# Modulation vectors of a two-block network: column groups of 1024, with the sums over the partitions begun by 32x32 transposes on VectorE

## The chip, the cores and the metric

One core of a Trainium2 chip runs the whole program in one launch. The time is the device time of one execution in microseconds (us), and the median of the runs counts. The engines are named as in the profile: PE is TensorE's matmul, PEld its weight load, DVE is VectorE, ACT is ScalarE, POOL is GpSimd, SP is SyncE, whose queue issues all the loads of weights.

## What is computed

The reference is a two-block residual network on 256 tokens of x (and 256 tokens of a context) with 1024 features, all in float32. Before every mixing or feed-forward stage the input is normalised and then modulated by vectors that come from a conditioning vector:

```
m = silu(cond) @ w_mod + b_mod          # first block: [1024] x [1024, 3072]
shift, scale, gate = split(m, 3)        # second block: [1024] x [1024, 9216], two layers, 9 vectors each
pre(h) = rms_norm(h, gain) * (1 + scale) + shift
h = h + gate * mixer(pre(h))
```

There are two conditioning vectors, one for x (`c`, `c_2`) and one for the context (`c_ctx`, `c_ctx_2`), so each product has two rows. The first block mixes with a chunked gated delta rule in both directions and a pooling branch. The second block has, for each of two layers, a feed-forward part (`ffn`, weight 0.5 on its gate), a mixer (a short convolution in layer 0, latent attention in layer 1) and another feed-forward part. The context leaves the computation after layer 1's attention has read its keys and values, so the last four modulation vectors of layer 1, and the gate of the first block, are used for x alone.

## The kernel before, in words

Activations lie transposed: features on the partitions, tokens in the free dimension (256 of x, then 256 of the context). A float32 product is made of three products of two-part operands (`mm3`, lines 220 to 223), each part `float32r`; every weight chunk of 128 x 2048 float32 (1 MB) is loaded as it is (`wraw`) and split into two parts (`whl`) by ACT (line 150) and DVE (line 151).

The work is a list of steps in `Program` (lines 64 to 155), each with the chunks that it uses. `pump` hands out raw buffers and split buffers in the order of the steps. In the second block there are two raw buffers (`wraw`) and four pairs of split buffers. A chunk that is not split, as those of `w_mod` are, keeps its raw buffer until its step has read it. After that a planner (the Tile framework's scheduler, line 1874) puts the instructions of each engine in an order by readiness in its own model of times; each engine then runs its own list in that order.

The modulation vectors are made by `mod_group` (lines 257 to 310), 512 columns at a time. A group is two steps, one per 512 rows of `w_mod`, so one 1 MB chunk each. A step runs in one of two ways:

- `by_pe` (lines 261 to 278): 16 products of 128 columns, with silu(c) as 32 stationary columns; four of them lie side by side in the array. The second step copies the sums to SBUF on ACT (tile `modsb`) and transposes them on PE, and two small DVE instructions add the bias.
- `by_dve` (lines 280 to 307): the products are left as 128 partial sums on the partitions. For each of four rows of weights and both conditioning vectors a `scalar_tensor_tensor` of 512 columns multiplies and adds into `macc` (the first two of a group are done by ACT, line 289). The second step then sums over the partitions on PE with four products of `ones` (line 298, tile `ps_mod`), copies to SBUF on ACT (line 300, `modsb`), transposes twice on PE (line 303, tile `ps_tr`) and adds the bias with two small DVE instructions (line 307).

PSUM has eight banks (line 171): four for products (`mm`), two that fill in (`fl`), one for small things (`tr`) and one for modulation (`mod`). The bank `mod` is also taken by the sums of the queries' squares in the first block (`T["ssq"]`, line 941, held from `q_step` 0 to `q_rows`) and by the second block's norms.

`mod_steps` (lines 349 to 357) takes the next steps from the queue `mod_q` and puts them into the list. There are 76 of them: 4 of the first block's gate and 72 of the second block. They are put

- two behind the solver of the first block (line 935) and ten into the scan over x (line 1142), by PE;
- one behind each `up` step of a feed-forward part whose context is still there (line 1392) and behind every second `down` step of its first half (line 1365), by DVE, until eight are left: 56 steps, in 28 groups;
- the last eight into the attention (line 1707), by PE.

An `up` step (lines 1317 to 1329) is 48 products of 512 columns into two banks, whose evacuation (`evac_g`, lines 1293 to 1299) uses the tiles `fs` and `fg` with two buffers each. A `z_step` of the first block (lines 999 to 1006) is 24 products into a bank `fl`; its result goes to the tile with the tag `X`, which was the scratch of the query steps before it (`Yw`, lines 967 and 968).

Of the kernel before, what the change touches and what calls it, by code (L numbers as in the profile page):

```python
# [14 lines left out]
P = 128  # L15
# [11 lines left out]
# columns of the packed per-feature vectors  # L27
# [12 lines left out]
class Chunk:  # L40
    """A piece of a weight matrix: n columns of float32 per partition, as the matrix product
    takes them (raw) or split into two float32r parts."""
# [7 lines left out]
class Slices:  # L50
    """A pool of [128, 256] tiles in slices of one tile."""
# [12 lines left out]
class Program:  # L64
    """Steps in their order, each with the weight pieces it uses; the pieces are loaded and split
    ahead of the steps, as far as there are buffers."""
# [10 lines left out]
    def add(self, fn, *chunks, lead=False):  # L77
        """lead: the step's instructions come before the splits that have room with it."""
        self.steps.append((fn, chunks, lead))
# [29 lines left out]
    @contextmanager  # L109
    def queued(self, behind):  # L110
        """Instructions that come behind these on their engines."""
        with ExitStack() as order:
            for ins in behind:
                order.enter_context(self.tc.issue_after(ins))
            yield
# [43 lines left out]
def adaln_net(ctx: ExitStack, tc: tile.TileContext, I, out):  # L159
# [13 lines left out]
    def bank(tag="mm"):  # L173
        """A bank by its use: products, fillers between them, small things, modulation;
        in the second block the first two in turn."""
# [33 lines left out]
    def into_row(h):  # L209
        """[128, 128], ones in the columns 64 + h and 96 + h: sums over partitions into those rows."""  # L210
        return rowsel[:, 7 - h:7 - h + P]

    def from_row(r):
        """[128, 128], ones in the row r: spreads that row over all partitions."""
        return ident[:, r:r + 1].to_broadcast([P, P])
# [41 lines left out]
    def mod_group(src, czt, dst, bias):  # L257
        """512 columns as 2 steps, one per 512 rows of w_mod."""
        st = {}

        def by_pe(c, ch):
# [3 lines left out]
            for k in range(4):  # L265
                for j in range(4):
                    o = k * 512 + j * P
                    mm(ps[32 * j:32 * j + 32, 0:P], czt[:, 4 * c + k, :], ch.raw[:, o:o + P],
                       c == 0 and k == 0, c == 1 and k == 3)
            if c == 0:  # L270
                return
            sb = const.tile([P, S], F32, tag="modsb", name="modsb")
            nc.scalar.activation(out=sb[:, 0:P], in_=ps[:, 0:P], func=AF.Copy)
            tr = side_bank()
            transpose(tr[:, 0:P], sb[:, 0:P])
            i0 = tr[:, 0:P].rearrange("p (j s) -> p j s", s=32)
            for r in range(2):
                tt(dst[:, :, r], i0[:, :, r], bias, ALU.add)

        def by_dve(c, ch):  # L280
            if c == 0:
                st["acc"] = T["scr"].tile([P, 2, 512], F32, tag="macc", bufs=1, name="macc")
            acc = st["acc"]
            for k in range(4):
                w = ch.raw[:, k * 512:(k + 1) * 512]
                for r in range(2):
                    cv = czt[:, 4 * c + k, r:r + 1]
                    if c == 0 and k == 0:
                        nc.scalar.activation(out=acc[:, r, :], in_=w, func=AF.Copy, scale=cv)  # L289
                    else:  # L290
                        stt(acc[:, r, :], w, cv, acc[:, r, :], ALU.mult, ALU.add)
            if c == 0:
                return
            ps = bank("mod")
            for r in range(2):
                for j in range(2):
                    q = 32 * (2 * r + j)
                    mm(ps[q:q + 32, 0:S], ones[:, 0:32], acc[:, r, j * S:(j + 1) * S])
# [5 lines left out]
            i0 = tr[:, 0:S].rearrange("p (b r j s) -> p r j b s", b=2, r=2, s=32)  # L304
            o = dst.rearrange("p (j b) r -> p j b r", b=2)
            for r in range(2):
                tt(o[:, :, :, r], i0[:, r, :, :, 0], bias.rearrange("p (j b) -> p j b", b=2), ALU.add)

        for c in range(2):
            mod_q.append((c, by_pe, by_dve, st, Chunk(src[c], 2048, split=False)))  # L310

    def mod_first(g):
        """Shift and scale of two tiles of the features."""
# [29 lines left out]
    for j in range(2):  # L343
        mod_group(I["w_mod_b"][j], cz["1"], mods["1"][:, 16 + 4 * j:20 + 4 * j], vec("b_mod", 16 + 4 * j, 4))
    for i in range(2):
        for j in range(18):
            mod_group(I["w_mod2"][i, j], cz["2"], mods[f"2{i}"][:, 4 * j:4 * j + 4], vec("b_mod_2", 72 * i + 4 * j, 4))
# [11 lines left out]
    def token_sums(out_, x, start, stop):  # L359
        """Sums over the partitions of x [128, 128], by tokens on the partitions: a column."""  # L360
        mm(out_, x, ones[:, 0:1], start, stop)

    def by_token(out_, r):
        """Columns of r, one per 128 tokens, over all partitions with the tokens in a row."""
# [1514 lines left out]
```

## Time and profile before

| | |
|---|---|
| runs | 2118.60, 2118.64, 2121.05 us; median 2118.64 us |
| profiled execution: span from first to last instruction | 2119.8 us; its time with what lies around the span is not listed apart |
| PE busy | 2077.7 us, 98% |
| PEld busy | 1797.6 us, 85% |
| DVE busy | 1266.4 us, 60% |
| ACT busy | 840.3 us, 40% |
| POOL busy | 77.4 us, 4% |
| DMA | 311.74 MB, mean 147 GB/s |
| chain that ended last, by engine | PE 95%, DVE 2%, ACT 1%, DMA 1%, issue 1% |
| mean granted TensorE clock | 0.994 |

The busy times are unions of the instructions' durations on each engine. [...] The chain of waits follows the last instruction back to what released it; its pieces are given in order of time, each with its start and its length.

### The profile page before, as it was taken

The numbers are of one execution on the slowest core, as the hardware profiler recorded it, in microseconds if no ns is written. First come the engines' busy times: TensorE is split into PE (matmuls) and PEld (weight loads), VectorE is DVE, ScalarE is ACT, GpSimd is POOL, SyncE is SP. The second block draws the span as 40 slices with busy tenths as digits, with TensorE's granted clock in tenths as the row PEclk, the third lists the DMA queues.
The fourth block names the chain that finished last, engine by engine and source line by source line (L and its number), as shares of the span: only waits on it lengthen the run. The fifth ranks groups of instructions, "written<-read, shape, count | busy, mean of one in ns | idle before, by whom it ended". The sixth has DMA issues, their size and how long they took to land.

```text
span 2119.8 us, 32648 instructions
## 1 busy us (share of the span) xinstructions
PE 2077.7 (98%) x13601; PEld 1797.6 (85%) x13601; DVE 1266.4 (60%) x2115; ACT 840.3 (40%) x1447; POOL 77.4 (4%) x80
## 2 busy tenths in 40 slices
PE   6999799999999999999999999999999999999999
PEld 6989798998788788888987878898888889579999
DVE  4669756578676764644766667466543236456553
ACT  4675362364322333433433233343322235555442
POOL 0000000030000002001000000110000010001000
PEclk9999999999999999999999999999999999999999
DMA  8243625544544443232244544324432233324453
GB/s 334 85 146 141 201 95 219 180 144 154 188 164 178 177 148 121 102 117 100 102 157 169 183 175 173 136 100 169 140 138 99 75 99 119 139 81 166 163 197 112
DMA packets 75379, 311.74 MB, mean 147 GB/s; under 512 B 26672, under 2 KB 36304, under 8 KB 45152
## 3 DMA queue, kind: packets, MB, share of 16 engines
q1 hardware_dynamic: 75232, 309.66, 41.5%
q8 instruction: 107, 1.75, 0.3%
q14 instruction: 40, 0.33, 0.0%
HBM read 301.72 MB, written 7.91 MB: 146 GB/s over the span
## 4 chain that ended last, share of the span: by engine, by line
PE 95%; DVE 2%; ACT 1%; DMA 1%; issue 1%; SPq 0%; ACTq 0%; DVEq 0%
PE ps_mm L218 61%; PE ps_fl L218 29%; PE ps_mod L218 3%; PE ps_tr L218 1%; PE ps_tr L234 1%; DVE O L240 0%; ACT gbuf L769 0%; DMA hres<-in_xT_dram 0%; DMA raw<-lane_d 0%; DVE X L237 0%; DVE gbuf L240 0%; ACT off L777 0%; PE ps_mm L234 0%; DVE vT L237 0%; DVE acc L240 0%
## 5 line engine op out<-in xcount | busy, mean ns | idle before, releaser
L218 PE MATMUL ps_mm<-hnh,whl 128*128 128x512 f32 (+1 forms) x2496 | 666.9, 351 | 1.1 <-ACT hnh L420 1.1
L150 ACT ACTIVATE whl<-wraw 128x1024 fp32r<-128x1024 f32 (+1 forms) x421 | 387.8, 970 | 592.3 <-PE ps_mm L218 192.4
L151 DVE TENSOR_TENSOR whl<-wraw,whl 128x1024 fp32r<-128x1024 f32 (+1 forms) x421 | 464.5, 1140 | 177.4 <-ACT whl L150 171.9
L218 PEld LDWEIGHTS ps_mm<-hnh,whl 128*128 128x128 f32 x2496 | 441.7, 190 | 67.2 <-issue 6.6
L218 PE MATMUL ps_mm<-hnl,whl 128*128 128x512 f32 (+1 forms) x1248 | 433.6, 349 | 0.0
L218 PE MATMUL ps_fl<-hnh,whl 128*128 128x512 f32 (+1 forms) x1040 | 292.3, 358 | 0.0
L237 DVE SCALAR_TENSOR_TENSOR macc<-wraw,cz,macc 128x512 f32<-128x512 f32 x392 | 268.1, 747 | 27.0 <-ACT macc L289 21.1
L218 PEld LDWEIGHTS ps_mm<-hnl,whl 128*128 128x128 f32 x1248 | 236.8, 190 | 28.9
L218 PE MATMUL ps_mm<-gh,whl 128*128 128x512 f32 (+1 forms) x924 | 243.6, 350 | 0.0
L218 PEld LDWEIGHTS ps_fl<-hnh,whl 128*128 128x128 f32 x1040 | 187.5, 189 | 30.3 <-issue 2.5
L218 PE MATMUL ps_fl<-hnl,whl 128*128 128x512 f32 (+1 forms) x520 | 185.2, 357 | 0.0
L218 PEld LDWEIGHTS ps_mm<-gh,whl 128*128 128x128 f32 x924 | 163.0, 189 | 23.0 <-issue 0.8
L218 PE MATMUL ps_mm<-gl,whl 128*128 128x512 f32 (+1 forms) x462 | 161.3, 349 | 0.0
L218 PE MATMUL ps_fl<-gh,whl 128*128 128x512 f32 (+1 forms) x616 | 159.5, 345 | 0.0
L240 POOL TENSOR_TENSOR nacc<-nacc,nsq 128x256 f32<-128x256 f32 x72 | 73.4, 1035 | 1597.0 <-ACT nsq L390 1455.0
L240 DVE TENSOR_TENSOR fg<-fs,ps_mm 128x512 f32<-128x512 f32 (+1 forms) x67 | 39.0, 584 | 154.5 <-PE ps_mm L218 146.5
L218 PEld LDWEIGHTS ps_fl<-gh,whl 128*128 128x128 f32 x616 | 107.5, 190 | 15.3 <-issue 1.6
L218 PEld LDWEIGHTS ps_fl<-hnl,whl 128*128 128x128 f32 x520 | 98.3, 189 | 13.5
L218 PE MATMUL ps_fl<-gl,whl 128*128 128x512 f32 (+1 forms) x308 | 105.5, 344 | 0.0
L218 PEld LDWEIGHTS ps_mm<-gl,whl 128*128 128x128 f32 x462 | 87.5, 189 | 11.1
L1296 ACT ACTIVATE fs<-ps_mm 128x512 f32<-128x512 f32 (+1 forms) x67 | 34.3, 514 | 136.1 <-PE ps_mm L218 136.0
L237 DVE SCALAR_TENSOR_TENSOR hres<-ps_mm,hg,hres 128x256 f32<-128x256 f32 x68 | 30.5, 480 | 81.5 <-PE ps_mm L218 81.4
(397 smaller groups left out, 2402.7 us busy)
## 6 DMA issues: line engine op xcount, KB each, us to landing
wraw<-in_ffn_up_dram SPq DMA_DIRECT2D x88, 1024.0 KB, 4.8
wraw<-in_w_mod_dram SPq DMA_DIRECT2D x72, 1024.0 KB, 4.8
wraw<-in_ffn_down_dram SPq DMA_DIRECT2D x64, 704.0 KB, 4.0
wraw<-in_sc_in_dram SPq DMA_DIRECT2D x12, 1024.0 KB, 4.7
wraw<-in_w_mod_a_dram SPq DMA_DIRECT2D x8, 1024.0 KB, 7.2
wraw<-in_w_out_dram SPq DMA_DIRECT2D x8, 1024.0 KB, 5.3
wraw<-in_w_k_dram SPq DMA_DIRECT2D x4, 1024.0 KB
wraw<-in_w_v_dram SPq DMA_DIRECT2D x4, 1024.0 KB, 4.7
```

The costliest lines, as they stand in the source:

```text
L150: nc.scalar.activation(out=c.hi[:, a:b], in_=c.raw[:, a:b], func=AF.Copy)
L151: nc.vector.tensor_tensor(out=c.lo[:, a:b], in0=c.raw[:, a:b], in1=c.hi[:, a:b], op=ALU.subtract)
L218: nc.tensor.matmul(out_, lhsT, rhs, start=start, stop=stop)
L234: nc.tensor.transpose(out_, in_, ident)
L237: return nc.vector.scalar_tensor_tensor(out=out_, in0=in0, scalar=scalar, in1=in1, op0=op0, op1=op1)
L240: return (eng or nc.vector).tensor_tensor(out=out_, in0=a, in1=b, op=op)
L1296: nc.scalar.activation(out=s_, in_=ps1[:, cols], func=AF.Silu)
```

## The change

`mod_group` works on 1024 columns in four steps, one per 256 rows of `w_mod`; a chunk is still 1 MB. In `by_pe` a step is 8 products of 256 columns instead of 16 of 128. In `by_dve` a step is two rows of weights by one or two conditioning vectors, with instructions of 1024 columns. At the end of a group DVE transposes 32x32 blocks of the partial sums, 512 columns at a time, into a tile of the tag `fg`, and sums along the free dimension; one PE product with a constant (`sel4`, four identity matrices of 32 in each direction) adds the four quarters of the partitions, and four small DVE instructions on 32 partitions each add the bias. The groups whose context part is not used (`both=False`: the first block's gate, and the last four groups of layer 1) compute x alone. The eight steps in the attention are gone from there; the steps by DVE lie behind three of four `up` steps, behind every second `down` step of a first half, and now also behind each of the eight steps of the short convolution. The two steps behind the solver and the ten in the scan stay by PE. The tile `modsb` holds `sel4` and the sums `mR` in the second block. The host lays `w_mod` out for the new chunks.

```diff
-    def mod_group(src, czt, dst, bias):
+    def mod_group(src, czt, dst, bias, both=True):
         st = {}
+        W = 1024
+        nr = 2 if both else 1
         def by_pe(c, ch):
...
-            for k in range(4):
+            for k in range(2):
                 for j in range(4):
-                    o = k * 512 + j * P
-                    mm(ps[32 * j:32 * j + 32, 0:P], czt[:, 4 * c + k, :], ch.raw[:, o:o + P],
-                       c == 0 and k == 0, c == 1 and k == 3)
-            if c == 0:
+                    o = k * W + j * S
+                    mm(ps[32 * j:32 * j + 32, 0:S], czt[:, 2 * c + k, :], ch.raw[:, o:o + S],
+                       c == 0 and k == 0, c == 3 and k == 1)
+            if c < 3:
                 return
...
+        def by_dve(c, ch):
+            if c == 0:
+                st["acc"] = T["scr"].tile([P, 2, W], F32, tag="macc", bufs=1, name="macc")
+            acc = st["acc"]
+            for k in range(2):
+                w = ch.raw[:, k * W:(k + 1) * W]
+                for r in range(nr):
+                    cv = czt[:, 2 * c + k, r:r + 1]
+                    if c == 0 and k == 0:
+                        nc.scalar.activation(out=acc[:, r, :], in_=w, func=AF.Copy, scale=cv)
+                    else:
+                        stt(acc[:, r, :], w, cv, acc[:, r, :], ALU.mult, ALU.add)
+            if c < 3:
+                return
+            R = T["mR"]
+            for r in range(nr):
+                for e in range(2):
+                    x = T["scr"].tile([P, NT], F32, tag="fg", bufs=2, name="mT")
+                    nc.vector.transpose(out=x, in_=acc[:, r, e * 512:(e + 1) * 512])
+                    nc.vector.reduce_sum(out=R[:, r, e * 16:(e + 1) * 16],
+                                         in_=x.rearrange("p (b i) -> p b i", i=32), axis=AX.X)
+            ps = bank("mod")
+            o = ps[:, 0:32 * nr].rearrange("p (r t q) -> p q t r", r=nr, q=4)
+            mm(ps[:, 0:32 * nr], T["sel4"], R[:, 0:nr, :].rearrange("p r b -> p (r b)"))
+            for q in range(4):
+                p = slice(32 * q, 32 * q + 32)
+                tt(dst[p, :, 0:nr], o[p, q], bias[p].unsqueeze(2).to_broadcast([32, 8, nr]), ALU.add)
...
-        for c in range(2):
+        for c in range(4):
             mod_q.append((c, by_pe, by_dve, st, Chunk(src[c], 2048, split=False)))
...
-    for j in range(2):
-        mod_group(I["w_mod_b"][j], cz["1"], mods["1"][:, 16 + 4 * j:20 + 4 * j], vec("b_mod", 16 + 4 * j, 4))
+    mod_group(I["w_mod_b"], cz["1"], mods["1"][:, 16:24], vec("b_mod", 16, 8), False)
     for i in range(2):
-        for j in range(18):
-            mod_group(I["w_mod2"][i, j], cz["2"], mods[f"2{i}"][:, 4 * j:4 * j + 4], vec("b_mod_2", 72 * i + 4 * j, 4))
+        for j in range(9):
+            mod_group(I["w_mod2"][i, j], cz["2"], mods[f"2{i}"][:, 8 * j:8 * j + 8], vec("b_mod_2", 72 * i + 8 * j, 8),
+                      i == 0 or j < 5)
...
     def open_b2():
...
+        t = const.tile([P, 512], F32, tag="modsb", name="sel4")
+        T["sel4"], T["mR"] = t[:, 0:P], t[:, P:P + 64].rearrange("p (r b) -> p r b", r=2)
+        nc.sync.dma_start(out=T["sel4"], in_=I["sel4"])
...
     def down_all(chunks, x, nk, both, norm=None, store=False):
...
             if not stat and m % 2:
-                mod_steps(1, 8, pe=False)
+                mod_steps(1, pe=False)
...
     def ffn(i, f, both, norm=None, store=False, parts=(0, 1)):
...
                 pr.add(up(up_ch[j], j, both), up_ch[j])
-                mod_steps(1, 8, pe=False)
+                if j % 4 != 3:
+                    mod_steps(1, pe=False)
...
     def short_conv():
...
             pr.add(step(m, None), *[chs[c] for c in ids])
+            mod_steps(1, pe=False)
...
     def mla():
...
-        mod_steps(8)
```

## Rows read from the trace of the kernel before

**Rows 1.** The page's parts 1 and 2: busy us (share) xinstructions; granted clock.
```profile
PE 2077.7 (98%) x13601; PEld 1797.6 (85%) x13601; DVE 1266.4 (60%) x2115; ACT 840.3 (40%) x1447; POOL 77.4 (4%) x80
...
PEclk9999999999999999999999999999999999999999
```

**Rows 2.** Busy time by stretch, second block: length, engines' busy (xcount), PEclk, DMA share, GB/s.
```profile
485.00:640.00 155.00, 155.00 (x757) 127.26 (x756) 111.90 (x176) 51.98 (x78) 0.00 (x0) 1.00 0.49 174
...
860.00:1020.00 160.00, 160.00 (x770) 135.20 (x770) 70.56 (x90) 50.86 (x72) 10.43 (x11) 1.00 0.30 105
...
1040.00:1430.00 390.00, 390.00 (x1994) 324.53 (x1993) 259.89 (x408) 130.64 (x203) 12.64 (x12) 1.00 0.44 157
...
1790.00:1900.00 110.00, 110.00 (x775) 70.89 (x774) 60.03 (x136) 63.34 (x124) 0.00 (x0) 1.00 0.36 128
```

**Rows 3.** The chain of waits, two up steps with one group's end: start, length, what.
```profile
514.74 5.00 PE ps_mm L218 x21
519.74 0.22 PE ps_tr L234 x2
519.95 6.15 PE ps_mm L218 x27
526.10 10.88 PE ps_fl L218 x48
536.98 0.57 PE ps_mod L218 x8
537.55 5.00 PE ps_mm L218 x21
```

**Rows 4.** Tile ps_mod, products of ones: duration ns min/median/max, first and last start.
```profile
L218 PE MATMUL ps_mod<-macc,ones x224: 379/391/403, 514.1 to 1514.9; 128*32 128x256 f32 x112
```

**Rows 5.** PE by stretch in the attention: tile ps_mod alone, then modsb alone.
```profile
1790.00:1855.00 65.00, 11.45 (x256) 1.00 0.42 151
...
1790.00:1855.00 65.00, 1.26 (x4) 1.00 0.42 151
```

**Rows 6.** Timeline of PE in the attention: start, us, line, instructions.
```profile
1845.42 1.96 PE L218 MATMUL ps_mod<-wraw,cz 128*32 128x128 f32 x64
1847.31 1.16 PE L218 MATMUL ps_mm<-dg,mgl 128*128 128x128 f32 x8
```

**Rows 7.** DVE groups by form, 486 to 1850 us: count, busy, mean ns, idle before.
```profile
L237 DVE SCALAR_TENSOR_TENSOR macc<-wraw,cz,macc 128x512 f32<-128x512 f32 x392 | 268.1, 747 | 27.0 <-ACT macc L289 21.1 <-DMA wraw<-in_w_mod_dram 5.9
L151 DVE TENSOR_TENSOR whl<-wraw,whl 128x1024 fp32r<-128x1024 f32 x214 | 256.0, 1227 | 119.2 <-ACT whl L150 118.0
L240 DVE TENSOR_TENSOR gl<-fg,gh 128x512 fp32r<-128x512 f32 x60 | 41.2, 687 | 6.6 <-ACT gh L226 6.6
...
L1609 DVE RECIPROCAL mgl<-mgl 128x512 f32<-128x512 f32 x1 | 3.3, 3339 | 0.0
...
L1660 DVE TENSOR_REDUCE mx<-ps_fl 128x1 f32<-128x512 f32 x2 | 1.4, 688 | 2.1 <-PE ps_fl L218 2.1
```

**Rows 8.** Timeline of the second block: a weight split, and the step that uses it.
```profile
572.44 2.35 DVE L151 TENSOR_TENSOR whl<-wraw,whl 128x1024 fp32r<-128x1024 f32 x2
...
583.11 0.50 PE L218 MATMUL ps_mm<-hnh,whl 128*128 128x512 f32 x1
```

**Rows 9.** Timelines of SP and PE in the first block's scan over the context.
```profile
304.84 15.65 SPq L132 DMA_DIRECT2D wraw<-in_w_mod_b_dram  x2
...
317.21 3.11 PE L218 MATMUL ps_fl<-hnx,whl 128*128 128x256 f32 x24
...
322.26 1.81 PE L218 MATMUL ps_fl<-hnx,whl 128*128 128x256 f32 x13
```

**Rows 10.** The page's part 6, loads of w_mod: count, KB each, us to landing.
```profile
wraw<-in_w_mod_dram SPq DMA_DIRECT2D x72, 1024.0 KB, 4.8
```

**Rows 11.** PE's longest idle time: timeline row, and the stretch around it.
```profile
249.56 2.50 PE L218 MATMUL ps_fl<-dp,whl 128*128 128x256 f32 x10 [9.38 <-DVE dp L240]
...
240.00:260.00 20.00, 10.47 (x173) 9.30 (x172) 14.89 (x16) 2.48 (x3) 3.78 (x4) 0.74 0.80 177
```

More of the change, by code (lines that the diff above doesn't have):

```diff
@@ L264, in by_pe @@
             ps = st["ps"]
-            for k in range(4):
+            for k in range(2):
                 for j in range(4):
-                    o = k * 512 + j * P
-                    mm(ps[32 * j:32 * j + 32, 0:P], czt[:, 4 * c + k, :], ch.raw[:, o:o + P],
-                       c == 0 and k == 0, c == 1 and k == 3)
-            if c == 0:
+                    o = k * W + j * S
+                    mm(ps[32 * j:32 * j + 32, 0:S], czt[:, 2 * c + k, :], ch.raw[:, o:o + S],
+                       c == 0 and k == 0, c == 3 and k == 1)
+            if c < 3:
                 return
[L272 to L295, printed above, removed]
-                for j in range(2):
-                    q = 32 * (2 * r + j)
-                    mm(ps[q:q + 32, 0:S], ones[:, 0:32], acc[:, r, j * S:(j + 1) * S])
             sb = const.tile([P, S], F32, tag="modsb", name="modsb")
@@ L303, in by_dve @@
                 transpose(tr[:, b * P:(b + 1) * P], sb[:, b * P:(b + 1) * P])
[L304 to L307, printed above, removed]
-        for c in range(2):
+            i0 = tr[:, 0:S].rearrange("p (b j s) -> p j b s", b=2, s=32)
+            for r in range(nr):
+                tt(dst[:, :, r].rearrange("p (j b) -> p j b", b=2), i0[:, :, :, r],
+                   bias.rearrange("p (j b) -> p j b", b=2), ALU.add)
+        def by_dve(c, ch):
[13 more added lines that the diff above has]
+            R = T["mR"]
+            for r in range(nr):
+                for e in range(2):
[10 more added lines that the diff above has]
+        for c in range(4):
             mod_q.append((c, by_pe, by_dve, st, Chunk(src[c], 2048, split=False)))
@@ L341, in mod_first @@
             pr.add(step(half, ch), ch)
-    for j in range(2):
-        mod_group(I["w_mod_b"][j], cz["1"], mods["1"][:, 16 + 4 * j:20 + 4 * j], vec("b_mod", 16 + 4 * j, 4))
+    mod_group(I["w_mod_b"], cz["1"], mods["1"][:, 16:24], vec("b_mod", 16, 8), False)
     for i in range(2):
-        for j in range(18):
-            mod_group(I["w_mod2"][i, j], cz["2"], mods[f"2{i}"][:, 4 * j:4 * j + 4], vec("b_mod_2", 72 * i + 4 * j, 4))
+        for j in range(9):
+            mod_group(I["w_mod2"][i, j], cz["2"], mods[f"2{i}"][:, 8 * j:8 * j + 8], vec("b_mod_2", 72 * i + 8 * j, 8),
+                      i == 0 or j < 5)
     def mod_steps(n, left=0, pe=True):
@@ L1824, in _layout @@
     o["cst"], o["msk"] = _consts()
+    o["sel4"] = np.tile(np.eye(32, dtype=np.float32), (4, 4))
     tok = lambda a: np.ascontiguousarray(a[0].T.reshape(KD, P, S).transpose(1, 0, 2))
@@ L1828, in _layout @@
     o["w_mod_a"] = np.ascontiguousarray(wm[:, 0:2048].reshape(2, 4, P, 2, 4, 256).transpose(4, 0, 2, 1, 3, 5)).reshape(4, 2, P, 2048)
-    cols = lambda w: np.ascontiguousarray(w.reshape(2, 4, P, -1, 512).transpose(3, 0, 2, 1, 4)).reshape(-1, 2, P, 2048)
-    o["w_mod_b"] = cols(wm[:, 2048:])
+    cols = lambda w: np.ascontiguousarray(w.reshape(4, 2, P, -1, 1024).transpose(3, 0, 2, 1, 4)).reshape(-1, 4, P, 2048)
+    o["w_mod_b"] = cols(wm[:, 2048:])[0]
     o["w_mod2"] = np.stack([cols(w) for w in x["w_mod_2"]])
```

## The prediction

> **What bounds the kernel now.** I read the page first. Its part 1 has PE busy 98% of a span of 2119.8 us, DVE 60%, ACT 40%, and the clock digits are full throughout [rows 1]. An average hides stages, so the table by stretches came next: in the second block PE is busy for all of each stretch, 155.00 us of 155, 160 of 160, 390 of 390, 110 of 110, at clock 1.00, while DVE has 111.9 of 155 us in the first feed-forward part, 259.9 of 390 in the later two and 70.6 of 160 in the short convolution [rows 2]. The reader is to see that nothing makes PE wait there: time goes away only if instructions leave PE, and work put on DVE is free as long as it keeps no weight split and no bank from PE.
>
> How much PE time a group's end takes can't be read from durations. The four products of ones are 224 records of 391 ns, 87.6 us in all [rows 4]; but the chain passes a group's end, eight records, in 0.57 us, since four column strips run side by side [rows 3]. The two transposes take 0.22 us there. The better measure is the period: from 514.74 to 537.55 us, 22.81 us, PE does two up steps of 48 products and one group's end. An undisturbed step is 10.88 us [rows 3], so the end costs 22.81 - 2 x 10.88 = 1.05 us, the slower products around the switches included.
>
> **The change part by part.** All against the profiled execution; its span of 2119.8 us is 1.2 us above the median of the runs, 2118.64 us, and I take the difference off the median.
>
> 1. Group ends by DVE lose four products, the copy and two transposes. 28 x 1.05 = 29.4 us leave PE [rows 3]. Bounds 28 x 0.79 = 22.1 (the two pieces of the chain alone) and 29.4. I take 29.4, as it is the period that the time is made of.
>
> 2. They gain one product with a constant: 16 group ends (64 steps by four), two records each of at most 64 columns with 128 stationary columns. No row shows it. The nearest are two transposes of 128 columns, 0.22 us: 16 x 0.22 = 3.5 us. The far end is the whole old end, 16 x 1.05 = 16.8. The switch between kinds of products must be paid as before, so I take 0.5 us each, 8 us.
>
> 3. The eight steps in the attention leave PE. Their records keep PE busy 11.45 us and their transposes 1.26 [rows 5], so at most 12.7 us go. Some of it fills holes: between 1845.42 and 1847.31 us 64 of these products stand just before the products with `dg`, which need the softmax of the scores [rows 6]; without them PE may wait for that. Nothing if all of it was filling. The rest of the attention, without such steps, has PE busy 110 of 110 us [rows 2], so I take 8 us as gone.
>
> 4. The twelve steps that stay by PE, in the first block, stream the same columns in half as many products: 0, bounds 0 and 3 us of gain.
>
> 5. DVE. Before: 392 instructions of 512 columns at 747 ns, 293 us, and 56 small ones [rows 7]. After: 12 groups with both vectors have 14 instructions of 1024 columns, four groups with x alone seven, 196 in all. 512 more columns cost 1227 - 687 = 540 ns, the difference of the subtractions of 1024 and of 512 columns, so each takes 747 + 540 = 1287 ns: 252 us, 41 us less [rows 7]. Added are 56 transposes and 56 sums over 512 columns. The sum is the reduction's row, 688 ns. No row shows a 32x32 transpose; the rows of that size lie between 687 ns and a reciprocal's 3339 ns [rows 7], and I take 0.69, an ordinary pass over one input. 56 x 1.38 = 77 us, so DVE gains some 36 us, all in stretches with 30 to 55% of it free [rows 2]: nothing on the path, unless it comes as a lump in the wrong place. A lump is 4 x 1.38 = 5.5 us, up to 16.1 us by the far end. What is queued behind it on DVE are the evacuations of up steps and the splits of weights; PE waits for those. A split now ends at 572.44 + 2.35 = 574.79 us for a step that starts at 583.11 [rows 8]: 8.3 us of cover. The short convolution takes two whole groups, some 2 x 23.5 = 47 us, onto 70.6 of 160 us, 74%. I take 3 us of lost time for all of this, between 0 and the slower rival below.
>
> [...]
>
> 6. A wait that the words of the change don't name. The two steps behind the solver used to be a whole group; now they are half of one, and its bank `mod` stays taken until the two steps in the scan over x have been done. The queries' sums want that only bank in between (line 941). The other two chunks are loaded behind the weights of z: the issues stand at 304.84 and 304.84 + 15.65 - 0.33 = 320.16 us [rows 9], and a load lands 4.8 us later [rows 10], so the bank comes free at about 326 us. Until then no query sum is made, the scratch with the tag `X` isn't given up, and the z steps, which write to that tag, can't be evacuated: two of them fit into the two banks `fl`, the step at 317.21 being the second, and the one at 322.26 [rows 9] has to wait until about 330. The products are done later, but the scan over the context has nothing else to fill PE with. The hole is between 0 (the scan's own products fill it) and 10 us; I take 4.
>
> 7. The loads: 76 of 1 MB as before; 64 KB for the constant. No load is near the path, DMA is at 0.30 to 0.49 [rows 2]. ACT loses the copies to `modsb` and the wait for the products of ones. 0.
>
> Sum: -29.4 + 8 - 8 + 0 + 3 + 4 = -22.4 us: 2118.64 - 22.4 = **2096 us**.
>
> **The rivals.**
>
> *All of it is gained* (0.14). The new product is at its low end, the attention gives all, and neither new wait is seen: -29.4 + 3.5 - 12.7 = -38.6, at best 2080; with a little less of each, about 2084. For it: PE has no idle time in any of these stretches [rows 2]. Against it: rows 6.
>
> *Given back* (0.12). The new product costs as much as the old end does (16.8 us), the attention gives nothing, and the bank's hole is 10 us: -29.4 + 16.8 + 10 = -2.6; with the 3 us of part 5, 2119. For it: switches between kinds of products do cost PE time [rows 3], and the bank is a real conflict. Against it: all three ends must meet.
>
> *Slower: PE starves behind group ends* (0.11). The four transposes take their buffers from the tag `fg`, which has two and which the evacuation of every up step also uses, and `macc` has one buffer. If the planner lets the transposes wait for the evacuation of the step before them, up to a whole step of 10.88 us [rows 3], then the next group's sums start behind the lump, the raw buffer of their chunk stays taken, and the split behind it is late by 10.88 + 5.5 us against a cover of 8.3. It decides when a split is over 8.3 us late at most group ends; 22.4 / 16 = 1.4 us of PE idle per group end beyond that eat the whole gain. At 3 us each the time is 2096 + 48 = 2144. Against it: three of four up steps instead of all carry a chunk now, and ACT and DVE no longer wait for products of ones. [...]
>
> [...]
>
> That the change doesn't do what it says: twelve steps stay by PE, and each group end keeps one product there; both are in the sum.
>
> **How the numbers follow.** My forecast has 0.63, with a range of its own from 2087 to 2110; the rivals 0.14, 0.12 and 0.11. The range for 8 in 10 takes in the forecast, nearly all of the first rival and the better third of the second: 2078 to 2115. A measurement of this kernel can tell 0.2%, 4.2 us, from no change. Faster by more is the forecast, the first rival and some of the second: 0.82. Within 0.2%, most of the second: 0.07. Slower: the third: 0.11.
>
> **What would show it.** In the chain of the changed kernel a period of two up steps and a group's end, once 22.81 us, should be 21.76 + 0.5, with one short piece of ps_mod and none of ps_tr. The steps in the short convolution should stay at their length. PE should still be busy all through 485 to 1900 us; idle time of PE with a weight split or a bank as its releaser, at every fourth mod step, would be the third rival. Idle time between 320 and 335 us, and z steps behind 330, would be part 6. In the attention the products with `dg` should follow the scores; a wait of theirs for ACT or DVE is the filled hole. A transpose of far more than 0.7 us on DVE would make part 5 wrong, and a clock below 1.00 behind 490 us the forecast with it.

## The result, and the profile after

The changed kernel takes 2088.48 us (median, 2086.42 to 2089.35, 4 runs), beside 2119.85 us of the kernel before in the same series: ratio 0.9848, 95% interval 0.9836 to 0.9860. Two later series gave 2087.66 and 2087.96 us. So it is faster by 1.5%, inside the range of 2078 to 2115 and 7.5 us better than the 2096 us that were forecast. The direction and the mechanism were right. Of the sum, only the largest term was right in size; the others were off, and the errors are told below one by one.

The profiled execution has a span of 2084.6 us, 35.2 us less than before. Its line of busy PE:

```profile
PE 2040.4 (98%) x12901; PEld 1778.7 (85%) x12901; DVE 1312.7 (63%) x2024; ACT 823.6 (40%) x1382; POOL 75.9 (4%) x80
```

Against [rows 1], PE has 700 records less and 37.3 us less to do, as much as the difference of the spans and 2 us more; the share stays at 98%. DVE has 91 instructions less but 46 us more busy time. The stretches that answer to [rows 2] (length, busy time by engine, clock, DMA share, GB/s):

```profile
485.00:640.00 155.00, 155.00 (x733) 130.36 (x732) 114.19 (x140) 47.23 (x63) 0.00 (x0) 1.00 0.47 167
...
860.00:1020.00 160.00, 159.48 (x807) 136.35 (x805) 114.89 (x161) 60.01 (x87) 10.30 (x12) 1.00 0.39 139
...
1040.00:1430.00 390.00, 390.00 (x1892) 330.17 (x1891) 259.99 (x339) 125.23 (x179) 12.62 (x12) 1.00 0.44 158
...
1790.00:1900.00 110.00, 105.57 (x608) 78.61 (x607) 58.46 (x124) 53.08 (x98) 7.10 (x6) 0.98 0.15 51
```

PE is as full as before up to the attention: the 0.5 us missing from 860 to 1020 us are a wait for `nsq` of a norm, which the trace of before has too, somewhat later. The short convolution carries the new DVE work, 114.89 of 160 us against 70.56; by the starts of its products it is 0.5 us longer than before, which is two group ends. The last stretch is less than full, 105.57 of 110 us, but not all of that is new. As everything comes 35 us earlier, the norm behind the attention now falls into it. To this norm belong 2.6 of the 4.4 us and the clock of 0.98: before, it lies at 1920 to 1940 us (PE busy 17.37 of 20 us, clock 0.91), now at 1880 to 1900 us, with the same two numbers. So this clock below 1.00, which the prediction named as a sign against itself, is no new loss. New are 1.8 us of idle time in this stretch and 0.8 just before it, both in the attention.

The chain that answers to [rows 3] (start, length, what), a group's end and the three up steps around it:

```profile
552.99 0.23 PE ps_fl L218
553.22 0.17 PE ps_mod L218 x2
553.39 10.72 PE ps_fl L218 x47
564.11 21.76 PE ps_mm L218 x96
```

From 552.99 to 564.11 us is 11.12 us for an up step of 10.88 with a group's end in it: the end costs 0.24 us, where it cost 1.05 [rows 3]. Two up steps without one still take 21.76. `ps_tr` is gone from the chain.

Where the 35.2 us went is read from the starts of the same products in both traces. Behind the first block, at 480 us, the new kernel is 4.7 us ahead; before the attention, at 1760 us, 30.3; behind it 35.3, and so to the end. Second block up to the attention: 25.6. Attention: 5.0. Two more profiles of the changed kernel, from the runs below, say how firm that is: from 480 to 1760 us the three agree within 0.1 us, but at 480 us they lie up to 2.1 us apart. So 25.6 is firm, and 4.7 only to some 2 us.

DVE's new instructions (busy us, mean ns, idle before them), beside [rows 7]:

```profile
L237 DVE SCALAR_TENSOR_TENSOR macc<-wraw,cz,macc 128x1024 f32<-128x1024 f32 x196 | 243.0, 1280 | 52.8 <-DMA wraw<-in_w_mod_dram 39.7 <-ACT macc L295 12.2
...
L304 DVE STREAM_TRANSPOSE mT<-macc 128x512 f32<-128x512 f32 x56 | 38.8, 700 | 0.0
L305 DVE TENSOR_REDUCE sel<-mT 128x16 f32<-128x512 f32 x56 | 37.2, 676 | 0.9
```

1280 and 700 ns against estimates of 1287 and 690: DVE's sizes were read rightly from their neighbours.

### The profile page after: what moved, and what is told of

Its sections match the earlier page's. It is cut to its first block, busy times and chain, and to the rows that moved or that the text cites. A ratio compares the mean times of both kernels' runs of the same rounds, so it can differ in the third digit from the quotient of the medians.

```text
span 2084.6 us, 31060 instructions
## 1 busy us (share of the span) xinstructions
PE 2040.4 (98%) x12901; PEld 1778.7 (85%) x12901; DVE 1312.7 (63%) x2024; ACT 823.6 (40%) x1382; POOL 75.9 (4%) x80
## 4 chain that ended last, share of the span: by engine, by line
PE 93%; DVE 3%; ACT 2%; DMA 1%; issue 1%; SPq 0%; ACTq 0%; DVEq 0%
PE ps_mm L218 61%; PE ps_fl L218 29%; PE ps_mod L218 2%; PE ps_tr L218 0%; ACT whl L150 0%; DVE O L240 0%; ACT gbuf L774 0%; DVE whl L151 0%; DMA raw<-lane_d 0%; DMA hres<-in_xT_dram 0%; DMA wraw<-in_w_q_dram 0%; DVE X L237 0%; DVE gbuf L240 0%; DVE vT L237 0%; PE ps_mm L234 0%
## 5 line engine op out<-in xcount | busy, mean ns | idle before, releaser
L237 DVE SCALAR_TENSOR_TENSOR macc<-wraw,cz,macc 128x1024 f32<-128x1024 f32 x196 | 243.0, 1280 | 52.8 <-DMA wraw<-in_w_mod_dram 39.7
L226 ACT ACTIVATE gh<-fg 128x512 fp32r<-128x512 f32 (+1 forms) x94 | 51.0, 545 | 139.7 <-DVE fg L240 139.7
```

Source lines behind the costliest of these rows:

```text
L226: a = nc.scalar.activation(out=hi, in_=src, func=AF.Copy)
L237: return nc.vector.scalar_tensor_tensor(out=out_, in0=in0, scalar=scalar, in1=in1, op0=op0, op1=op1)
```

## The experiments

Theory A: in the second block time is PE's instructions; what leaves PE is gained, and DVE's work is free. Theory B: the gain comes from ACT and DVE no longer waiting for PE at a group's end, or from another order of the list. The changed kernel itself was run again as a yardstick, in the first series and in the last; the series between them (lump, closed group, groups of 512, first block as before) is compared through the kernel before, which ran in all three.

> The changed kernel once more, as the measure for the others on the same chip. Both theories: 2088 us, between 2086 and 2091, ratio to the kernel before 0.985.

2087.66 us (2085.56 to 2089.41), ratio 0.9846 [0.9833, 0.9859].

### Wide groups alone

```diff
-            R = T["mR"]
...
-            mm(ps[:, 0:32 * nr], T["sel4"], R[:, 0:nr, :].rearrange("p r b -> p (r b)"))
...
+            for r in range(nr):
+                for j in range(4):
+                    mm(ps[32 * j:32 * j + 32, r * S:(r + 1) * S], ones[:, 0:32], acc[:, r, j * S:(j + 1) * S])
+            sb = const.tile([P, 512], F32, tag="modsb", name="modsb")
+            nc.scalar.activation(out=sb[:, 0:nr * S], in_=ps[:, 0:nr * S], func=AF.Copy)
+            tr = side_bank()
+            for b in range(2 * nr):
+                transpose(tr[:, b * P:(b + 1) * P], sb[:, b * P:(b + 1) * P])
...
```

> Groups of 1024 columns stay, but a group's sums over the partitions are made by products of ones, a copy and transposes on PE again. Theory A (in the second block the time is PE's instructions): a group with both vectors has 16 records of ones and four transposes, about 1.1 + 0.44 + 0.26 = 1.8 us, 12 of them, four groups with x alone 1.05 us each, 25.8 us in all, less 16 x 0.2 of the products with the constant: 2088 + 22 = 2110 us. Theory B (the gain comes from ACT and DVE no longer waiting for PE, and from another order of the lists): the wait of the accumulators for PE comes back, which B also prices, but PE's time doesn't count: below 2095 only if the waits didn't matter either. Between 2104 and 2115 is A.

2111.0 us (2107.73 to 2121.62), ratio 0.9969 [0.9954, 0.9984]: 23.3 us of the changed kernel's gain are gone. Four of the 12 runs stand apart, at 2119.37 us and above, with a mean granted clock of 0.989 or 0.990 against 0.994 to 0.996 in the others; without them the median is 2109.7 us. Such upper levels come again below. The profiled execution is of the lower level. Its chain of waits has the two pieces of a group's end on PE again:

```profile
541.49 1.00 PE ps_mod L218 x16
542.49 5.48 PE ps_mm L218 x23
547.98 0.44 PE ps_tr L234 x4
```

Between 480 and 1760 us it loses 21.3 us against the changed kernel: 1.50 us at each of the 12 ends with both vectors, PE's pieces of 1.44 us less the 0.17 of the product and 0.23 around them, and 0.82 us at each of the four with x alone. With the product's 0.24 us an end of x alone then costs 1.06 us, and the same instructions cost 1.05 by the period in the kernel before. That is theory A, in the numbers of rows. The transposes on VectorE are the change; the wider groups with their ends left on PE, four of them for x alone, keep 4.3 of the 25.6 us.

### The last steps in the attention again

```diff
     def down_all(chunks, x, nk, both, norm=None, store=False):
...
-                mod_steps(1, pe=False)
+                mod_steps(1, 8, pe=False)
...
     def ffn(i, f, both, norm=None, store=False, parts=(0, 1)):
...
-                    mod_steps(1, pe=False)
+                    mod_steps(1, 8, pe=False)
...
     def short_conv():
...
-            mod_steps(1, pe=False)
+            mod_steps(1, 8, pe=False)
...
     def mla():
...
+        mod_steps(8)
```

> Only the last eight steps go back into the attention, by PE (two groups of x alone). Theory A with holes (the stage came out 4.9 us shorter): 2088 + 4.9, less two products with the constant, about 2093 us. If all PE time of these steps counts (the prediction's upper bound, 12.7 us): 2100. If they only fill holes: 2088.

2093.09 us, ratio 0.9873 [0.986, 0.9886]: 5.4 us more, theory A's number. In the profiled execution the attention is 7.0 us longer, and the two group ends that are gone from before it give 0.6 back. PE's work there was up to 12.7 us [rows 5], so part of it had cost nothing. Some of it had filled holes, which are seen in the changed kernel (timeline of PE, in brackets the idle time and its releaser):

```profile
1770.84 1.04 PE L218 MATMUL ps_mm<-mgl,cst 128*32 128x512 f32 x2 [0.57 <-ACT mgl L1611]
...
1802.45 0.74 PE L218 MATMUL ps_mm<-cq,identr 128*128 128x512 f32 x2 [0.59 <-DVE kn L240]
...
1804.78 1.12 PE L218 MATMUL ps_fl<-kn,mgh 128*128 128x512 f32 x2 [1.00 <-DVE kn L240]
```

None of these gaps was in the trace of before. With two of 0.23 and 0.21 us they come to 2.6 us; the other 5 us or so are not holes, and no run places them in full. The forecast's words (a wait for ACT or DVE) came true, at `kn` and `mgl`, not at the products with `dg`.

### The product with the constant five times

```diff
-            mm(ps[:, 0:32 * nr], T["sel4"], R[:, 0:nr, :].rearrange("p r b -> p (r b)"))
+            for _ in range(5):
+                mm(ps[:, 0:32 * nr], T["sel4"], R[:, 0:nr, :].rearrange("p r b -> p (r b)"))
```

> The product with the constant is made five times at each group end, the result being the same. Theory A with the chain's 0.17 us for its two records: 16 x 4 x 0.17 = 11 us more, 2099 us. With the 0.5 us that the prediction took for each: 32 us more, 2120. Theory B (PE's time is hidden): 2088.

2111.42 us, ratio 0.9945 [0.9924, 0.9965], 23.8 us more, between theory A's two numbers and far from theory B's 2088; but the runs lie on two levels, two at 2101.28 and 2103.68 and four from 2111.26 to 2112.96. The profiled one is of the upper level. Its chain prices the product:

```profile
552.47 1.06 PE ps_mod L218 x10
```

1.06 - 0.17 = 0.89 us for four more, 0.22 us each; 16 ends are 14.2 us, and 2087.7 + 14.2 = 2101.9 us is the lower level. The other 10 us stand in the attention: up to 1800 us this execution is 13.5 us behind the changed kernel's, from 1830 us on 24.9. There its clock is at half (length, busy time by engine, clock, DMA share, GB/s):

```profile
1820.00:1840.00 20.00, 20.00 (x28) 6.47 (x28) 6.64 (x21) 3.47 (x8) 0.00 (x0) 0.50 0.09 37
```

The same step of 11.3 us is in the groups of 512 below.

### The lump three times as long

```diff
                     x = T["scr"].tile([P, NT], F32, tag="fg", bufs=2, name="mT")
-                    nc.vector.transpose(out=x, in_=acc[:, r, e * 512:(e + 1) * 512])
...
+                    for _ in range(3):
+                        nc.vector.transpose(out=x, in_=acc[:, r, e * 512:(e + 1) * 512])
+                        nc.vector.reduce_sum(out=R[:, r, e * 16:(e + 1) * 16],
+                                             in_=x.rearrange("p (b i) -> p b i", i=32), axis=AX.X)
```

> The changed kernel with every 32x32 transpose and the sum behind it done three times: 112 more transposes of 705 ns and 112 more sums of 680 ns, 155 us of DVE and not one PE instruction more. At a group's end DVE has 12 x 1.385 = 16.6 us in place of 5.5, against the 8.3 us of cover that the trace of before showed for a weight split. Theory A (the second block's time is PE's instructions, DVE's work is free while splits and evacuations keep coming): 2087.7 us as the changed kernel, up to 2092. Rival (the lump stands in front of the splits): each of the 12 full ends makes a split 16.6 - 8.3 = 8.3 us late, 12 x 8.3 = 100 us, or some 20 us if the planner breaks up most of the lump: 2108 to 2188, with PE idle time whose releaser is DVE whl.

2112.8 us (2104.75 to 2117.64), ratio 0.9962 [0.9948, 0.9975]. The profiled execution is one of the faster, 2106.91 us, and no trace shows what the slower ones add. In it neither theory holds for all ends: 14 of 16 group ends cost nothing, two cost about 10 us each. PE's waits in the second block (us in total, times, longest), and one of the two on DVE, ACT and PE:

```profile
PE ps_mm L218 <- ACT whl L150: 14.6, 2, 7.5
```
```profile
673.47 1.25 DVE L306 TENSOR_REDUCE sel<-mT 128x16 f32<-128x512 f32 x2
674.62 0.69 DVE L240 TENSOR_TENSOR fg<-fs,ps_mm 128x512 f32<-128x512 f32 x1
675.22 0.71 DVE L305 STREAM_TRANSPOSE mT<-macc 128x512 f32<-128x512 f32 x1
```
```profile
675.35 0.63 ACT L226 ACTIVATE gh<-fg 128x512 fp32r<-128x512 f32 x1 [2.23 <-DVE fg L240]
675.97 2.19 ACT L295 ACTIVATE macc<-wraw,cz 128x1024 f32<-128x1024 f32 x2
...
684.44 2.00 ACT L150 ACTIVATE whl<-wraw 128x1024 fp32r<-128x1024 f32 x2 [2.34 <-DMA wraw<-in_ffn_up_dram]
```
```profile
685.55 0.80 PE L218 MATMUL ps_mm<-hnh,whl 128*128 128x512 f32 x1 [7.51 <-ACT whl L150]
```

This is the third rival's path, but for its first link: there the transposes wait for an evacuation, here an evacuation waits for the transposes. Its `fg` stands on DVE behind transposes and sums that began at 662.76 us. The next group's first instruction on ACT, at 675.97, stands behind the `gh` that needs this `fg`; it also writes `macc`, of which there is only one buffer and which the last transpose reads until 675.93, so the trace does not say which of the two held it. From there on the path is one: the chunk of `w_mod` keeps its raw buffer, the load of weights that wants this buffer is issued at 679.67 us (the same load of the changed kernel at 666.49), and PE waits 7.51 us for their split. The other hole, at 1232 us, is 7.11 us; the remaining 5 us or so of the 20 lost are slower products behind the holes, where the granted clock is 0.83 and 0.74 over 20 us.

So the rival was a real mechanism, and it begins to cost somewhere between one and three times the present lump. In the changed kernel PE waits for no weight split between 485 and 1900 us.

### The group in the first block closed

```diff
     pr.add(solve_out)
-    mod_steps(2)
+    mod_steps(4)
```

> The changed kernel with all four steps of the first block's gate behind the solver, so that no group is open and the bank mod is free when the queries' sums want it. Same instructions on every engine, in another order. Theory A (PE's instructions alone): 2087.7 us. If the open bank costs what the prediction gave it: 2087.7 - 4 = 2084, and the queries' sums move from 326 us to some 300 us. If the order of the list around the hole of 9.39 us behind dp matters more: two more steps by PE of some 1.1 us each stand in or around that hole, 2 us either way.

2085.46 us (2085.17 to 2088.1), ratio 0.9843 [0.983, 0.9855], against the changed kernel's 0.9846 in the series before: not told apart. The sums of the queries in the changed kernel, then here (durations, then first and last start):

```profile
L218 PE MATMUL ps_mod<-ones,Yw x32: 169/250/271, 326.1 to 335.8; 128*128 128x1 f32 x32
```
```profile
L218 PE MATMUL ps_mod<-ones,Yw x32: 168/250/271, 265.1 to 312.9; 128*128 128x1 f32 x32
```

The bank did what part 6 said, to the microsecond: 326. The hole did not come. From 315 to 352 us the changed kernel's only wait of PE is 0.28 us: products of the scan (`V,kt`, `q,kv`, `hres,kv`) stand there, and the z steps just come later (337.48 us). In the stretch around it PE is busy alike, the changed kernel first, then this one:

```profile
320.00:412.00 92.00, 90.60 (x839) 78.85 (x838) 50.73 (x128) 30.35 (x57) 0.00 (x0) 1.00 0.52 191
```
```profile
320.00:412.00 92.00, 90.60 (x879) 80.01 (x879) 57.06 (x137) 31.79 (x56) 0.00 (x0) 1.00 0.58 207
```

By the starts this execution gains 1.2 to 2.1 us between 224 and 480 us on the three profiles of the changed kernel. So the open bank, with the order that comes with it, costs some 2 us at most.

### Groups of 512 columns on DVE

```diff
+    def mod_group512(src, czt, dst, bias, both):
...
+                x = T["scr"].tile([P, NT], F32, tag="fg", bufs=2, name="mT")
+                nc.vector.transpose(out=x, in_=acc[:, r, :])
+                nc.vector.reduce_sum(out=R[:, r, 0:16], in_=x.rearrange("p (b i) -> p b i", i=32), axis=AX.X)
...
+        for j in range(0 if i else 4, 18):
+            mod_group512(I["w_mod2s"][i, j], cz["2"], mods[f"2{i}"][:, 4 * j:4 * j + 4], vec("b_mod_2", 72 * i + 4 * j, 4),
+                         i == 0 or j < 10)
```

> The changed kernel with 512 columns to a group wherever the sums are made on DVE: 32 group ends in place of 16, each with one transpose and one sum per vector and a product with the constant of half as many columns; the instructions that multiply and add are 512 columns wide, 747 ns each, so that DVE has some 41 us more. Theory A: 16 more ends of at most 0.24 us on PE, 3.8 us, so 2091 us: nearly all of the gain is the transposes', not the wider group's. Rival (the width gives the gain, by fewer ends, fewer DVE instructions and later release of buffers): half of the gain goes, 2104 us.

2095.34 us (2091.99 to 2100.52), ratio 0.989 [0.9874, 0.9906]. From 480 to 1780 us it loses 3.8 us, as theory A said (16 more ends of 0.24). The rest is again the attention. The gaps there are the changed kernel's (0.58, 0.59 and 1.00 us), but the clock falls in this execution. First the changed kernel, then this one (columns as above, the clock is the third number from the end):

```profile
1800.00:1810.00 10.00, 8.41 (x22) 3.22 (x21) 8.87 (x17) 1.56 (x4) 0.00 (x0) 1.00 0.29 105
1810.00:1820.00 10.00, 10.00 (x38) 4.64 (x38) 5.34 (x19) 4.44 (x10) 0.00 (x0) 1.00 0.00 0
```
```profile
1800.00:1810.00 10.00, 8.41 (x24) 3.83 (x22) 9.31 (x14) 2.28 (x4) 0.00 (x0) 0.84 0.30 105
1810.00:1820.00 10.00, 10.00 (x11) 2.50 (x10) 3.24 (x10) 2.59 (x6) 0.00 (x0) 0.50 0.01 2
1820.00:1830.00 10.00, 10.00 (x18) 3.86 (x17) 2.43 (x10) 2.24 (x6) 0.00 (x0) 0.50 0.00 0
```

At the granted 0.50, from some 1808 to 1831 us, the same pairs of products take 2.00 us from one start to the next in place of 1.06, 11.3 us more in all. Without that it would stand near theory A's 2091 us, as two of its runs do, at 2092 and 2093.3 us.

### The first block's twelve steps as before

`mod_group512` is here the `mod_group` of the kernel before with its `by_pe` alone.

```diff
-    mod_group(I["w_mod_b"], cz["1"], mods["1"][:, 16:24], vec("b_mod", 16, 8), False)
+    for j in range(2):
+        mod_group512(I["w_mod_b"][j], cz["1"], mods["1"][:, 16 + 4 * j:20 + 4 * j], vec("b_mod", 16 + 4 * j, 4))
+    for j in range(4):
+        mod_group512(I["w_mod2s"][j], cz["2"], mods["20"][:, 4 * j:4 * j + 4], vec("b_mod_2", 4 * j, 4))
```

> The changed kernel with the twelve steps by PE in the first block (gate, and the first 2048 columns of layer 0) as they were before: 512 columns to a group, products of 128 columns, two steps to a group; the second block as in the changed kernel. Theory A for the first block (its 4.7 us come from half as many products on PE in the twelve steps): 2087.7 + at most 3 = 2090.7 us, spread over the twelve steps. Rival (the 4.7 us come from the order of the list, that is from less idle time and less time at the half clock around 265 us): 2092.4 us, and PE idle for some 3.9 us there, with the first block's length back at 466.4 us.

2092.4 us (2090.39 to 2097.8, 4 runs), ratio 0.9877 [0.9861, 0.9892]: the rival's number, though the run at 2097.8 us has a clock of 0.988 and the other three alone would give 2091.24. Until 230 us it is about 1 us behind the changed kernel's first profile, behind the first block 6.1; between these points it loses 3.9 to 4.8 us, by which of the three profiles of the changed kernel it is set against. The old hole is back. The changed kernel's first, then this one's:

```profile
269.57 1.29 PE L218 MATMUL ps_tr<-Yw,off 32*32 32x32 f32 x128 [1.64 <-ACT TT L1001]
```
```profile
267.87 0.97 PE L218 MATMUL ps_tr<-TT,tmp 32*32 32x32 f32 x90 [3.85 <-issue]
```

So the first block's 4.7 us come with the other shape of the groups, around the solver's end. They are mostly the clock behind the holes, not the idle time itself. From 225 to 480 us PE is idle for 13.4 us in the kernel before and 13.1 us in the changed one; but from 225 to 300 us the granted clock is 0.86 before and 0.91 after, and 0.05 of 75 us is 3.8 us, an estimate, of the 4.2 us gained there. In this run the clock is 0.89, and PE is idle for 14.6 us. How much the order of the list does for it, and how much the products, half as many and twice as wide, this run does not part; that theory A's bound of 3 us is passed speaks for the order.

### Filling the gaps, the yardstick again, and a better order

> The changed kernel once more, beside the two others of this series. 2087.7 us. In e5_groups_512 and e6_const_x5 the profiled executions fell to a granted 0.50 between some 1808 and 1830 us in the attention, behind the gaps of 0.59 and 1.00 us before the products with kn, and lost 11 us by it; the changed kernel has the same gaps and had 1.00 there in both profiles. If that is chance, some of its executions stand 10 us above the others, at about 2098; if it can't happen here, all lie within 2085 to 2090.

2087.96 us (2085.67 to 2090.24), ratio 0.9852 [0.9839, 0.9866]. In its 12 runs so far, the first four among them, the changed kernel never stands on an upper level. Neither does the closed group in its five. Other kernels without PE's steps in the attention do, at a mean clock of 0.988 to 0.990 and 6 to 10 us above their other runs: wide groups alone in 4 of 12, the product five times in 4 of 6, the groups of 512 in 2 of 5, the first block as before in 1 of 4. (The long lump has holes of its own and can't be counted so.) The kernel before, which has such steps, has none in its 45 runs of the three series, where the lowest mean clock is 0.993; nor has the kernel with the steps put back in its four.

The next one is the product five times together with the steps in the attention, the edits of the two experiments above.

> e6_const_x5 with the last eight steps by PE in the attention again: the product with the constant five times at 14 group ends, and 128 products of 256 columns and their ends between the products with kn. Theory (the gaps that the removed steps left bring TensorE's clock down in some executions, which is what spread e6_const_x5 from 2101 to 2113 us): 2087.7 + 5.4 for the steps + 14 x 0.89 = 2105.6 us in all runs, within 3 us of each other, clock at 1.00 all through the attention. Rival (the clock falls for another reason): two levels again, 2105 and 2116 us, and a granted 0.50 behind 1800 us in the profile if it is one of the later.

2105.9 us (2105.75 to 2109.18, 5 runs), ratio 0.9941 [0.9929, 0.9953]: one level, at the number expected. With PE's steps back, the five gaps are gone, one of 0.54 us at 1830.64 us is new, and the clock stays up:

```profile
1810.00:1830.00 20.00, 20.00 (x109) 9.95 (x107) 13.25 (x22) 7.69 (x12) 0.00 (x0) 1.00 0.63 229
```

With the counts of runs (an upper level in four of six without these steps, in none of five with them) it bears out that the clock falls behind the gaps, though the steps put back also change what PE does around them. Why the changed kernel, with the same gaps, kept 1.00 in each profile is open.

The last one tries for more, at the longest wait that both kernels have once PE has begun [rows 11] (before PE's first product there are 14.4 and 14.1 us), with one line of `solve_out` edited on top of the closed group:

```diff
-        with pr.queued(T["pool", 2]):
+        with pr.queued(T["pool", 3]):
```

> e4_group_closed with one more edit in the first block: the five DVE instructions that write the solver's result O (8.16 us in one piece) are put behind the last pooling product instead of the last but one, so that the last dp, for which PE waits 9.39 us at 238.8 us in the changed kernel and 6.3 + 1.5 us in e4_group_closed, stands before them on DVE. If that wait was time: up to 7.9 us less than e4_group_closed's 2085.5, 2078 us. If the chain behind O (its store, its load, the transposes of Yw) sets the time there: the same wait is found behind O, 2085 us or up to 3 us more.

2091.55 us (2088.7 to 2103.57), ratio 0.9889 [0.9866, 0.9911]: 3.6 us above the changed kernel and worse than both numbers expected, with two of six runs on an upper level. PE's longest waits from 225 to 300 us:

```profile
PE ps_mm L234 <- ACT kt L1030: 3.5, 1, 3.5
PE ps_tr L218 <- DMA Yw<-sol_d: 2.9, 1, 2.9
PE ps_mod L218 <- ACT Yw L951: 2.2, 1, 2.2
PE ps_tr L218 <- ACT TT L1001: 1.7, 1, 1.7
```

The wait for `dp` is gone. Of these, that for `TT` was there in the changed kernel (1.6 us); the other three are new and stand around the solver's later result. PE is idle for 11.8 us here and for 11.2 in the changed kernel, and the granted clock is 0.84 in place of 0.91. Behind the first block the profiled execution is 3.5 us later than that of the closed group alone. The 9.4 us were cover for that chain. No version here is told apart from the changed kernel on the better side.

## Why the prediction came out as it did

| step | forecast | measured | by |
|---|---|---|---|
| 1 and 2: group ends, less the new product | -29.4 + 8 | -25.6 | the starts at 480 and 1760 us |
| 3: attention | -8 | -5.0 | the starts; 5.4 by medians with the steps put back |
| 4 and 6: first block | 0 + 4 | -4.7 | the starts at 480 us; 2092.4 with the old steps |
| 5: DVE | +3 | 0 | no PE wait for a split |
| sum | -22.4 | -35.3 | the starts; 35.2 by the spans |

By medians the gain is 31.4 us (2119.85 - 2088.48), not 35.2, as the table compares one execution of each kernel. That of the changed kernel is the fastest of its four runs, 2.1 us below their median. That of before has a span of 2119.8 us; with the 1.8 us that lie around the span in the changed kernel (2086.42 - 2084.6) it took some 2121.6 us, an estimate, 1.8 above the median. The prediction set its span against the median of times and took the difference for 1.2 us.

That 2088.48 us also lies in the forecast's own range, from 2087 on, is partly luck: steps 2, 4, 5 and 6 all erred to the slow side, by 15.9 us together, step 3 to the other by 3.0, and the measured terms would give 2118.64 - 35.3 = 2083.3 us.

**Steps 1 and 2.** The price by the period was right: 28 x 1.05 less 16 x 0.24 is 29.4 - 3.8 = 25.6 us, the number measured. What failed is the size of step 2: 0.5 us for a product that costs 0.24 with all that is around it, on the argument that a switch between kinds of products must be paid as before. The nearest row, two transposes in 0.22 us, was the better guide. The old end had 0.26 us around its two pieces (1.05 - 0.79), and the ends on PE in the experiment with wide groups have 0.23; the new one has 0.07 (0.24 - 0.17). The mis-sizing is 4.2 us.

**Step 3.** 5.0 of 12.7 us, inside the bounds; 8 was too much by 3. The holes, 2.6 us in five gaps, were known to be possible from [rows 6], but not where they would open. Part of the rest is the method: 12.7 us is busy time, and from the start of each run of these products and transposes to the start of the product behind it they take some 10.9 us in the trace of before. The remaining 3 us or so stay open, and so does why the steps cost 7.0 us in their new form, when they are put back.

**Step 4.** Here the sign was wrong: with step 6 the first block was to lose 4 us, and it gained 4.7, more than step 4's bound of 3. By the experiment with the old steps the gain comes around the solver's end, where the clock is higher (0.91 against 0.86 over 75 us). That the halved products, or groups closed at other steps, shift what the list puts there is argued; a sum over instructions can't see it.

**Step 5.** The lump stays within its cover, and DVE's new load in the short convolution costs PE nothing beyond the group ends. DVE has 46 us more to do where 36 were forecast: the forecast took 41 us off for the wider instructions by adding up recorded durations (293 - 252), but these overlap, and by busy time it is 268.1 - 243.0 = 25 us. No time hung on it. The estimate of 5.5 us for the lump is even a little long, as the records of DVE's instructions overlap: in the kernel with the long lump two transposes start 1.22 us before what follows them, 0.61 each, though one is recorded with 0.70 or more.

**Step 6.** The place and the moment were right, the price was not: some 2 us at most in place of 4, and no hole, as the scan had other products for PE. "The scan has nothing else to fill PE with" is the sentence that failed.

**The rivals.** "All of it is gained" (2084) was nearer than the forecast, and two of its three reasons held: the product is at its low end (3.8 us), and neither new wait is seen. The third did not: the attention gave less than half, and the first block, which it left out, made up for it. "Given back" fell with the price of the product. Starvation behind group ends did not happen, and tripling the lump showed that its path exists.

## What to carry to other kernels

Where one engine is full, price a piece of its work by the period with and without it, not by its records, and price its substitute by the nearest row of the same shape rather than by analogy with what it replaces. Work given to a second engine was free here (46 us more on DVE, no wait of PE for a split) until a buffer that the first one needs was held behind it (waits of 7.51 and 7.11 us with the lump three times as long); test that by making the work three times as long, not by its share of busy time. When work leaves a stage that it was filling, look at the gaps it leaves: here gaps of 2.6 us in all were followed in two profiled executions by a granted 0.50 that cost 11.3 us.

## What the hardware showed that was not expected

- Gaps of about 0.6 and 1.00 us before the products with `kn` were followed by 23 us at 0.50 of the clock in two profiled executions (11.3 us lost), those of the groups of 512 and of the product five times. They were followed by none in eight others with the same gaps, the three of the changed kernel among them; its busy time of PE there is equal to that of the groups of 512 (8.41 of 10 us). The 0.74 around the longer gap of [rows 11] agrees that gaps matter; what decides between the two outcomes no run here shows.
- A product with 128 stationary and 64 moving float32 columns, repeated, costs 0.22 us, about the same as a product of two `float32r` operands with 512 columns (0.227 us, 10.88 us over 48).
